# Attention heads of a hybrid layer: head output summed by VectorE from its bank, at other steps; query copy and key part moved by a step; value weights loaded in the fifth head

## The chip, the cores and the metric

The kernel runs on one core of a Trainium2 chip. The metric is the device time of one execution in microseconds, median of the runs of one kernel; less is better. All five engines have their own instruction stream: PE (TensorE), DVE (VectorE), ACT (ScalarE), POOL (GpSimd) and SP (SyncE, which here only issues transfers).

## The reference

One backbone layer over 512 latent tokens of 1024 channels and 256 context tokens. A combined projection feeds two branches: an eight-head attention with low-rank queries and keys (branch A), and a bidirectional gated linear attention with four heads (branch B). Their outputs are merged, added to the residual, and followed by a gated MLP with a 3x3 depthwise convolution. The change lies in branch A:

```python
s = jnp.einsum('bqhd,bkhd->bhqk', qn, k_nope) + jnp.einsum('bqhr,bkr->bhqk', qr, k_rope)
p = jax.nn.softmax(s.astype(jnp.float32) * MLA_SCALE, axis=-1).astype(v.dtype)
return jnp.einsum('bhqk,bkhd->bqhd', p, v)
```

There are 768 keys (512 latent, 256 context), 512 queries and 8 heads of 64 + 32 channels, values of 64 channels.

## The kernel before

All products run in float32 quality with operands split into two parts (`hi`, and `lo` = value minus `hi`): `mm3` is three matmuls, hi by hi, hi by lo and lo by hi. A split is a copy on ScalarE (`A`) and a subtraction on GpSimd (`G`) or VectorE (`V`).

The attention loop runs over heads `h` and six steps `s`. In each step the TensorE queue gets: four transposes of probabilities for the next step (`turned`, into one of two banks, copied by ScalarE to `ph` and subtracted by VectorE to `pl`), then what `between(h, s)` puts in, then `weighed`, four matmuls of the values of step `s` into the head's output bank `po`. `po` is `single[2]` for even heads and `single[3]` for odd ones. Its 128 rows hold 64 rows of the hi part of the value product and 64 of the lo part; the head's output is the sum of both halves, written as hi and lo into the rows of the head in `oT[pr]` (two heads share one tile).

`between` does, in the order of the code: exponentials of the scores made in the step before (`exped`, ScalarE), the second half of the key copy for the next pair of heads (`key_parts(1)`, ScalarE and VectorE, step 5 of even heads), the scores of the next head (`scores`, six matmuls into one of two double banks, and a row maximum on VectorE), the query product of the head after it (`prep_q`, in step 5 of even and step 0 of odd heads), the output of the head before (`heads_out`), the normalisation of probabilities (`normed`, a reciprocal on VectorE and a product on GpSimd), the key product of the next pair (`keys`, step 3 of even heads), and pieces of later work. `wide()` hands out the two double banks `two[0]` and `two[1]` in turn: to scores, key products and the query product of odd steps.

`prep_q` is a product (`q_mm`), a multiplication by a table on VectorE into the buffer `X` (`q_table`), and a split of `X` (`q_parts`, subtraction on GpSimd). `X` has one buffer, and `heads_out` uses it too:

```python
A.copy(hi, po[rw, :])
rest = tl(e1, [128, 512], F32, "X", 1)
A.copy(rest[rw, :], po[ro, :])
sub(V, lo, po[rw, :], f(hi))
tt(G, lo, f(lo), rest[rw, :], ALU.add)
```

`gla_v_load` loads the value weights of branch B (four loads of 512 KB), `gla_v_split` splits an eighth of them; `gla_steps` lists the step of each eighth. In head 7 the value product of branch B (`gla_v`) fills TensorE, in the two double banks.

During the attention the instructions of TensorE, VectorE and ScalarE stand in the order of the code. GpSimd's order, SP's, and everything after the attention is chosen by a planner from times of its own. Which buffer a tile of a pool gets is decided there too; a tile whose buffer is still in use waits for it. The tiles `s` of the trace have 30 buffers, `raw` 3, `whi` and `wlo` 4 each.

In the trace nearly all instructions show the line of a helper (L88), so the names of tiles tell them apart: `p` are the double banks, `pb` the single ones, `mx` the maxima, `rs` the row sums, `kT` the keys, `P` and `raw` the probabilities.

Of the kernel before, what the change touches and what calls it, by code (L numbers as in the profile page):

```python
# [9 lines left out]
F32 = mybir.dt.float32  # L10
# [3 lines left out]
ALU = mybir.AluOpType  # L14
# [6 lines left out]
NH = 8  # L21
# [49 lines left out]
def block_kernel(ctx: ExitStack, tc: tile.TileContext, p, out):  # L71
# [3 lines left out]
    class Engine:  # L75
# [5 lines left out]
        def __getattr__(self, op):  # L81
            fn = getattr(self.eng, op)

            def call(*args, **kw):
                if self.name in behind:
                    with tc.issue_after(behind[self.name].ins):
# [6 lines left out]
    V, A, G, PE, SY = (Engine("V", nc.vector), Engine("A", nc.scalar), Engine("G", nc.gpsimd),  # L93
                       Engine("PE", nc.tensor), Engine("SY", nc.sync))
    cnt = [0]

    def tl(pool, shape, dt, tag, bufs=None):
        cnt[0] += 1
        kw = {} if bufs is None else {"bufs": bufs}
        return pool.tile(shape, dt, name=f"{tag}_{cnt[0]}", tag=tag, **kw)  # L100
# [8 lines left out]
    def pb():  # L109
        return tl(psp, [128, 512], F32, "pb", 4)  # L110

    def p2():
        return tl(psp, [128, 1024], F32, "p2", 2)

    def S4(shape, dt=F32R):
        return tl(s4, shape, dt, "s4")

    def S4f():
        return S4([128, 1024], F32)
# [10 lines left out]
    def f(ap):  # L130
        return ap.bitcast(F32)

    def tt(eng, out_, a, b, op):
        return eng.tensor_tensor(out=out_, in0=a, in1=b, op=op)

    def sub(eng, out_, a, b):
        eng.tensor_tensor(out=out_, in0=a, in1=b, op=ALU.subtract)
# [6 lines left out]
    def mm3(o, sh, sl, mh, ml, first, last):  # L144
        PE.matmul(o, lhsT=sh, rhs=mh, start=first, stop=False)
        PE.matmul(o, lhsT=sh, rhs=ml, start=False, stop=False)
        return PE.matmul(o, lhsT=sl, rhs=mh, start=False, stop=last)
# [4 lines left out]
    def k3(t_, k, n):  # L152
        return t_[:, 0:k * n].rearrange("p (k n) -> p k n", k=k)
# [163 lines left out]
    def tok(kt, t):  # L317
        return lat(kt, t * 128, 128) if t < 4 else cxt(kt, (t - 4) * 128, 128)
# [16 lines left out]
    with tc.tile_pool(name="e1", bufs=1) as e1:  # L335
# [118 lines left out]
        def decay_weights():  # L454

            r, wd2 = S4f(), S4([128, 2, 512])
            for d in range(2):
                SY.dma_start(out=r[64 * d:64 * d + 16, 0:512], in_=p["gla_w_decay"][0, d])
            for d in range(2):
                yield  # L460
                rw = slice(64 * d, 64 * d + 16)
                G.tensor_copy(wd2[rw, 0, :], r[rw, 0:512])
                yield
                sub(G, wd2[rw, 1, :], r[rw, 0:512], f(wd2[rw, 0, :]))
                for n in range(3):
                    SY.dma_start(out=f(wst)[64 * d + 16 * n:64 * d + 16 * n + 16, :], in_=f(wd2)[rw, n % 2, :])
# [17 lines left out]
        two, single = [p2(), p2()], [pb() for _ in range(4)]  # L484
# [229 lines left out]
        def wide():  # L714
            turn[0] += 1
            return two[turn[0] % 2]

        def q_mm(h, qp):
            for k in range(3):
                mm3(qp, wqh[k][:, h, :], wql[k][:, h, :], qch[k], qcl[k], k == 0, k == 2)  # L720

        def q_table(qp):
            X = tl(e1, [128, 512], F32, "X", 1)
            tt(V, X, qp, qtab, ALU.mult)
            return X

        def q_parts(h, X):
            q2 = S4([128, 2, 512])
            A.copy(q2[:, 0, :], X)
            sub(G if h else V, q2[:, 1, :], X, f(q2[:, 0, :]))  # L730
            q2s[h] = q2

        def q_out(h, qp):
            q_parts(h, q_table(qp))

        def prep_q(h, qp):
            q_mm(h, qp)
            q_out(h, qp)
# [11 lines left out]
        def key_parts(i):  # L750
            kp = kps[0][64 * i:64 * i + 64, 0:768]
            A.copy(kTh[i][0:64, :], kp)
            sub(V, kTl[i][0:64, :], kp, f(kTh[i][0:64, :]))
# [14 lines left out]
        def scores(h, n):  # L768

            i, q2 = h % 2, q2s[h]  # L770
            cs = slice(n * 128, (n + 1) * 128)
            sp = wide()
            for (a, b) in ((0, 512), (512, 768)):
                mm3(sp[:, a:b], q2[:, 0, cs], q2[:, 1, cs], kTh[i][:, a:b], kTl[i][:, a:b], True, True)
            mx, rs = sm(1, "mx", 4), sm(1, "rs", 4)
            V.tensor_reduce(out=mx, in_=sp[:, 0:768], op=ALU.max, axis=AX.X, negate=True)
            pt = EP() if n < 2 else raw_tile()[:, 0:768]
            P[h].append(pt)
            open_.append((pt, rs, sp, mx))

        def exped():

            for pt, rs, sp, mx in open_:
                A.activation(pt, sp[:, 0:768], AF.Exp, bias=mx, accum_out=rs)
            exped_.extend(open_)
            open_.clear()

        def normed(n=4):

            for pt, rs, sp, mx in exped_[:n]:  # L790
                V.reciprocal(rs, rs)
                G.tensor_scalar(out=pt, in0=pt, scalar1=rs, scalar2=1.0, op0=ALU.mult, op1=ALU.mult)
            del exped_[:n]

        def heads_out(h, po):
            i, pr = h % 2, h // 2
            if i == 0:
                oT[pr] = S4([128, 2, 512])
            rw, ro = slice(64 * i, 64 * i + 64), slice(64 - 64 * i, 128 - 64 * i)
            hi, lo = oT[pr][rw, 0, :], oT[pr][rw, 1, :]  # L800
            A.copy(hi, po[rw, :])
            rest = tl(e1, [128, 512], F32, "X", 1)
            A.copy(rest[rw, :], po[ro, :])
            sub(V, lo, po[rw, :], f(hi))
            tt(G, lo, f(lo), rest[rw, :], ALU.add)

        def turned(h, s):

# [22 lines left out]
        glav, wv, gps, glv, m0 = [], [], {}, [None], []  # L831
# [3 lines left out]
        def gla_v_load(i):  # L835
            graw.append(S4f())
            SY.dma_start(out=k3(graw[i], 2, 512), in_=w_in[:, 2 * i:2 * i + 2, CGV:CGV + 512])

        def gla_v_split(k):

            if k % 2 == 0:
                whl_[:] = whl()
            wv.append([w[:, k % 2 * 512:k % 2 * 512 + 512] for w in whl_])
            split(*wv[k], graw[k // 2][:, k % 2 * 512:k % 2 * 512 + 512])
# [3 lines left out]
        def gla_v(t, k0=0, k1=KT):  # L848
            if k0 == 0:
                if t % 2 == 0:  # L850
                    glav.append(S4([128, 2, 512], F32))
                gps[t] = two[t // 2][:, t % 2 * 512:t % 2 * 512 + 512] if t < 4 else pb()
            for k in range(k0, k1):
                sh, sl = tok(k, t)
                glv[0] = mm3(gps[t], sh, sl, *wv[k], k == 0, k == 7)
            if k1 == KT:
                A.copy(glav[t // 2][:, t % 2, :], gps[t])

        def between(h, s):

            n = ((0, 1, 2, None, 3, None), (None, 0, 1, 2, 3, None))[h % 2][s]
            exped()
            if h + 2 < NH and (h % 2, s) == (0, 5):
                key_parts(1)
            if h + 1 < NH and n is not None:
                scores(h + 1, n)
            if h + 2 < NH and s == (5, 0)[h % 2]:
                prep_q(h + 2, wide()[:, 0:512] if h % 2 else single[3])
            if h > 0 and s == h % 2:
                heads_out(*pend)  # L870
            normed()
            if h + 2 < NH and (h % 2, s) == (0, 3):
                keys(h // 2 + 1)
                key_parts(0)
            if h == 2:
                next(dw, None)
            if h == 5 and 1 <= s <= 4:
                gla_v_load(s - 1)
            for k in range(KT):
                if (h, s) == gla_steps[k]:  # L880
                    gla_v_split(k)
            if (h, s) == (1, 2):
                pinned.add("G")
                misc_parts()
                pinned.discard("G")
            if h == 0 and s < 2:
                values(4 + s, single[3])
                values_out(4 + s, single[3])
            if (h, s) == (6, 5):
                begun.append(mp_tile())  # L890
                m0.append(mod_steps(3072, begun[0], raw_tile))
                next(m0[0])
                behind["SY"] = load[0]
            if h == 7:
                gla_v(*gla_fill[s])
                for _ in range(2 if s else 0):
                    next(m0[0], None)

        dw = decay_weights()
        gla_steps = [(5, 5), (6, 0), (6, 3), (6, 3), (6, 4), (6, 4), (6, 5), (6, 5)]  # L900
        gla_fill = [(0, 0, 2), (0, 2, 4), (0, 4, 6), (0, 6, 8), (1, 0, 4), (1, 4, 8)]

        cb_ = [single[1][:, 0:256], single[1][:, 256:512]]
# [119 lines left out]
        for h in range(NH):  # L1023
            po = single[2 + h % 2]
# [381 lines left out]
    with tc.tile_pool(name="eff", bufs=1) as ef:  # L1406
# [82 lines left out]
        for t in range(4):  # L1489
# [8 lines left out]
            for i, (a, b) in enumerate(parts):  # L1498
# [11 lines left out]
                else:  # L1510

                    cs = slice(t * 128, (t + 1) * 128)
                    rest = pb()[:, 0:256]
# [48 lines left out]
```

## Time and profile before

| | |
|---|---|
| median of 3 runs | 916.47 us (916.03 to 918.38) |
| profiled execution | 919.78 us |
| its span, first to last instruction | 918.0 us |
| mean granted TensorE clock | 0.994 |
| busy share PE / DVE / ACT / POOL | 97% / 63% / 44% / 42% |

The span is what the instructions take from the first to the last; the profiled execution's own time has 1.78 us around it. The attention loop lies between about 103 and 221 us of the span. A granted clock of 1.00 is TensorE's upper level (2.4 GHz), 0.50 its lower one (1.2 GHz).

### The profile page before, as it was taken

The numbers are of one execution on the slowest core, as the hardware profiler recorded it, in microseconds if no ns is written. First come the engines' busy times: TensorE is split into PE (matmuls) and PEld (weight loads), VectorE is DVE, ScalarE is ACT, GpSimd is POOL, SyncE is SP. The second block draws the span as 40 slices with busy tenths as digits, with TensorE's granted clock in tenths as the row PEclk, the third lists the DMA queues.
The fourth block names the chain that finished last, engine by engine and source line by source line (L and its number), as shares of the span: only waits on it lengthen the run. The fifth ranks groups of instructions, "written<-read, shape, count | busy, mean of one in ns | idle before, by whom it ended". The sixth has DMA issues, their size and how long they took to land.

```text
span 918.0 us, 12643 instructions
## 1 busy us (share of the span) xinstructions
PE 889.5 (97%) x4864; PEld 751.7 (82%) x4864; DVE 574.8 (63%) x963; ACT 399.9 (44%) x663; POOL 382.0 (42%) x231
## 2 busy tenths in 40 slices
PE   5999999989999999999999999999999999999996
PEld 4878888878878888888887889888888888888885
DVE  4567877664977777775665584988687776400006
ACT  4355666683435454533546333343424333322105
POOL 4412356472434443333464422344435344476403
PEclk9999999999999999999999999999999999999998
DMA  9930000306232424143982612434343433254102
GB/s 320 336 111 1 1 4 9 92 25 203 61 81 61 124 51 134 37 137 105 294 264 83 184 46 69 138 103 146 97 137 92 138 99 108 69 160 139 46 1 92
DMA packets 131437, 100.89 MB, mean 110 GB/s; under 512 B 6827, under 2 KB 121875, under 8 KB 131377
## 3 DMA queue, kind: packets, MB, share of 16 engines
q1 hardware_dynamic: 130256, 97.56, 34.8%
q0 software_dynamic: 864, 2.22, 0.7%
q8 instruction: 38, 0.62, 0.3%
q10 hardware_dynamic: 256, 0.30, 0.1%
q14 instruction: 23, 0.18, 0.1%
HBM read 97.78 MB, written 2.10 MB: 109 GB/s over the span
## 4 chain that ended last, share of the span: by engine, by line
PE 86%; DVE 5%; ACT 4%; issue 2%; POOL 1%; DMA 1%; POOLq 0%; DVEq 0%; ACTq 0%
PE pb L88 45%; PE p L88 22%; PE pb L87 14%; PE p L87 6%; DVE s L88 1%; DVE kT L88 1%; POOL s L88 1%; ACT ph L88 1%; DMA raw<-in_w_ada_dram 1%; ACT P L88 1%; DVE mx L88 1%; ACT s L88 1%; ACT raw L88 1%; DVE X L88 1%; ACT kT L88 1%
## 5 line engine op out<-in xcount | busy, mean ns | idle before, releaser
L88 POOL TENSOR_TENSOR wlo<-raw,whi 128x1024 fp32r<-128x1024 f32 (+1 forms) x106 | 240.9, 2279 | 338.8 <-ACT whi L88 310.3
L88 PE MATMUL pb<-s,whi 128*128 128x512 f32 (+1 forms) x906 | 272.3, 383 | 0.0
L88 PEld LDWEIGHTS pb<-s,whi 128*128 128x128 f32 x906 | 167.6, 188 | 32.2
L88 ACT CAST whi<-raw 128x1024 fp32r<-128x1024 f32 (+1 forms) x106 | 103.3, 975 | 178.0 <-issue 77.3
L88 PE MATMUL pb<-s,wlo 128*128 128x512 f32 (+1 forms) x453 | 172.9, 382 | 0.0
L88 DVE SCALAR_TENSOR_TENSOR ac<-pb,cwT,ac 128x441 f32<-128x441 f32 (+2 forms) x160 | 111.0, 694 | 19.3 <-ACT ac L88 15.4
L87 PE MATMUL pb<-s,whi 128*128 128x512 f32 x320 | 101.8, 396 | 0.0
L88 PEld LDWEIGHTS pb<-s,wlo 128*128 128x128 f32 x453 | 85.3, 188 | 16.5
L88 PE MATMUL p<-s,s 128*128 128x512 f32 (+1 forms) x392 | 83.5, 369 | 1.7 <-DVE s L88 1.7
L88 PEld LDWEIGHTS p<-s,s 128*128 128x128 f32 x392 | 66.4, 191 | 15.0 <-DVE s L88 2.3
L88 PE MATMUL p<-whi,s 128*128 128x512 f32 x208 | 69.9, 397 | 1.0 <-ACT raw L88 0.9
L87 PEld LDWEIGHTS pb<-s,whi 128*128 128x128 f32 x320 | 58.9, 188 | 12.4 <-issue 0.7
L88 DVE TENSOR_TENSOR p<-p,gt 128x512 f32<-128x512 f32 x4 | 2.8, 699 | 98.5 <-PE p L88 98.4
L87 PE MATMUL pb<-s,wlo 128*128 128x512 f32 x160 | 62.8, 392 | 0.0
L88 PE MATMUL pb<-whi,s 128*128 128x512 f32 x176 | 57.5, 390 | 0.0
L88 PEld LDWEIGHTS p<-whi,s 128*128 128x128 f32 x208 | 39.5, 190 | 9.6 <-ACT raw L88 1.1
L88 DVE TENSOR_TENSOR pl<-pb,ph 128x512 fp32r<-128x512 f32 x48 | 33.0, 687 | 20.0 <-ACT ph L88 19.9
L88 PE MATMUL p<-kT,s 128*128 128x512 f32 (+1 forms) x192 | 41.2, 351 | 3.6 <-ACT P L88 3.6
L88 PE MATMUL pb<-s,s 128*32 128x128 f32 (+2 forms) x322 | 43.6, 335 | 1.1 <-DMA s<-in_w_ada_dram 1.1
L88 PE MATMUL p<-wlo,s 128*128 128x512 f32 x104 | 41.0, 394 | 0.0
L88 ACT ACTIVATE ac<-ac 128x512 f32<-128x512 f32 x22 | 13.9, 632 | 60.8 <-DVE ac L88 60.8
L88 PE MATMUL p<-s,whi 128*128 128x256 f32 (+1 forms) x156 | 39.1, 342 | 1.3 <-DVE kT L88 1.2
(252 smaller groups left out, 1561.7 us busy)
## 6 DMA issues: line engine op xcount, KB each, us to landing
raw<-in_w_up_dram SPq DMA_DIRECT2D x44, 512.0 KB, 3.8
raw<-in_w_in_dram SPq DMA_DIRECT2D x28, 512.0 KB, 3.9
raw<-in_w_down_dram SPq DMA_DIRECT2D x22, 512.0 KB, 3.7
s<-in_w_ada_dram SPq DMA_DIRECT2D x20, 512.0 KB, 5.7
raw<-in_w_ada_dram SPq DMA_DIRECT2D x18, 512.0 KB, 4.8
xn<-in_w_ada_dram SPq DMA_DIRECT2D x10, 512.0 KB, 5.7
kT<-in_w_in_dram SPq DMA_DIRECT2D x8, 320.0 KB, 6.8
s<-in_x_dram SPq DMA_DIRECT2D x4, 512.0 KB, 5.1
```

Of the source, the lines that this page charges most:

```text
L87: return fn(*args, **kw)
L88: ins = fn(*args, **kw)
```

## The change

`heads_out` no longer copies the second half into `X`: VectorE adds it straight from the bank. It is called in step 2 of even heads (it was 0) and step 0 of odd heads (it was 1). `key_parts(1)` stands ahead of the exponentials of its step. In odd heads the query product and the table product stay in step 0, behind `heads_out`, and the split of `X` moves to step 1. The loads of the value weights move from steps 1 to 4 of head 5 to steps 2 to 5 of head 4, their splits from (5,5) to (6,5) to (4,5) to (6,3). The value product takes the two double banks in the other order.

```diff
-            rest = tl(e1, [128, 512], F32, "X", 1)
-            A.copy(rest[rw, :], po[ro, :])
             sub(V, lo, po[rw, :], f(hi))
-            tt(G, lo, f(lo), rest[rw, :], ALU.add)
+            tt(V, lo, po[ro, :], f(lo), ALU.add)
...
-                gps[t] = two[t // 2][:, t % 2 * 512:t % 2 * 512 + 512] if t < 4 else pb()
+                gps[t] = two[1 - t // 2][:, t % 2 * 512:t % 2 * 512 + 512] if t < 4 else pb()
...
+            even = h % 2 == 0
+            if h + 2 < NH and even and s == 5:
+                key_parts(1)
             exped()
-            if h + 2 < NH and (h % 2, s) == (0, 5):
-                key_parts(1)
             if h + 1 < NH and n is not None:
                 scores(h + 1, n)
-            if h + 2 < NH and s == (5, 0)[h % 2]:
-                prep_q(h + 2, wide()[:, 0:512] if h % 2 else single[3])
-            if h > 0 and s == h % 2:
+            if h + 2 < NH and even and s == 5:
+                prep_q(h + 2, single[3])
+            if h + 2 < NH and not even and s == 1:
+                q_parts(h + 2, X_[0])
+            if h > 0 and s == (2, 0)[h % 2]:
                 heads_out(*pend)
+            if h + 2 < NH and not even and s == 0:
+                qp = wide()[:, 0:512]
+                q_mm(h + 2, qp)
+                X_[0] = q_table(qp)
             normed()
...
-            if h == 5 and 1 <= s <= 4:
-                gla_v_load(s - 1)
+            if h == 4 and s > 1:
+                gla_v_load(s - 2)
...
-        dw = decay_weights()
-        gla_steps = [(5, 5), (6, 0), (6, 3), (6, 3), (6, 4), (6, 4), (6, 5), (6, 5)]
+        dw, X_ = decay_weights(), [None]
+        gla_steps = [(4, 5), (5, 0), (5, 2), (5, 3), (5, 4), (5, 5), (6, 0), (6, 3)]
```

## Rows read from the trace of the kernel before

**Rows 1.** Part 1 of the profile page: busy us of each engine, its share of the span, instructions.

```profile
PE 889.5 (97%) x4864; PEld 751.7 (82%) x4864; DVE 574.8 (63%) x963; ACT 399.9 (44%) x663; POOL 382.0 (42%) x231
```

**Rows 2.** Busy time by stretches: the stretch and its length, then busy us (and instructions) of PE, PEld, DVE, ACT and POOL, the granted clock, the DMA share and GB/s. The cuts are the first transposes of odd heads and of head 6, the start of head 7, the first value matmul and the end of the lower clock; the last row is all after the attention.

```profile
120.25:148.17 27.92, 26.68 (x176) 23.70 (x175) 20.29 (x35) 19.11 (x36) 19.75 (x20) 1.00 0.05 11
148.17:176.11 27.94, 26.71 (x176) 23.73 (x175) 20.30 (x35) 19.10 (x36) 12.38 (x12) 1.00 0.13 38
176.11:189.62 13.51, 12.31 (x83) 10.92 (x82) 10.01 (x17) 8.02 (x16) 6.54 (x6) 1.00 0.25 78
189.62:201.71 12.09, 10.50 (x74) 9.29 (x73) 8.47 (x16) 11.11 (x23) 9.85 (x10) 1.00 0.15 46
201.71:203.19 1.48, 0.60 (x6) 0.36 (x4) 1.03 (x3) 1.32 (x4) 1.48 (x2) 1.00 0.02 6
203.19:206.71 3.52, 3.52 (x10) 2.94 (x11) 0.84 (x2) 1.46 (x3) 3.52 (x4) 0.52 0.00 0
235.00:918.00 683.00, 674.02 (x3410) 567.83 (x3408) 422.41 (x668) 264.85 (x402) 286.25 (x129) 1.00 0.37 111
```

**Rows 3.** Who waited for whom, weight loads of TensorE (PEld) from 118 to 204 us: us in total, times, longest.

```profile
PEld p L88 <- ACT P L88: 5.2, 8, 1.2
PEld p L88 <- DVE kT L88: 1.9, 3, 0.6
PEld p L88 <- ACT raw L88: 1.1, 1, 1.1
PEld pb L88 <- DVE pl L88: 0.5, 1, 0.5
PEld pb L88 <- ACT ph L88: 0.5, 1, 0.5
```

**Rows 4.** The chain of work that ended last, 146 to 160 us (from the end of head 2 to the scores of head 3): start, us, engine and tile.

```profile
146.31 1.00 ACT raw L88 x2
...
147.33 0.81 ACT kT L88
...
148.16 0.97 DVE kT L88
...
151.01 1.25 POOL s L88
...
155.05 0.58 ACT X L88
...
157.19 1.32 PE p L88 x6
```

**Rows 5.** TensorE in order of time, one step of head 3: start, us (the ends are modelled and overlap the next start), what; the first row of each group (transposes, query product, weighing, transposes, scores, weighing).

```profile
148.17 0.60 PE L88 MATMUL pb<-cst,P 128*128 128x128 f32 x4
149.17 0.74 PE L88 MATMUL p<-s,whi 128*128 128x512 f32 x2 [0.40 <-DVE kT L88]
...
151.38 0.28 PE L88 MATMUL pb<-ph,s 128*128 128x256 f32 x1
...
151.85 0.60 PE L88 MATMUL pb<-cst,P 128*128 128x128 f32 x4
152.21 1.30 PE L88 MATMUL p<-kT,s 128*128 128x512 f32 x6
153.34 0.29 PE L88 MATMUL pb<-ph,s 128*128 128x256 f32 x1
...
155.80 0.60 PE L88 MATMUL pb<-cst,raw 128*128 128x128 f32 x4
```

**Rows 6.** VectorE and GpSimd in order of time: a row maximum and the subtraction for the output of head 1 (136.12, 137.10; the output lies in the upper half of the partitions), the table product into X, a maximum, the subtraction for the output of head 2 (lower half) and the next instruction, and GpSimd's addition for that output.

```profile
136.12 0.95 DVE L88 TENSOR_REDUCE mx<-p 128x1 f32<-128x768 f32 x1
137.10 0.69 DVE L88 TENSOR_TENSOR s<-pb,s 64x512 fp32r<-64x512 f32 x1
...
152.30 0.69 DVE L88 TENSOR_TENSOR X<-p,qtab 128x512 f32<-128x512 f32 x1 [0.48 <-POOL s L88]
...
154.78 0.95 DVE L88 TENSOR_REDUCE mx<-p 128x1 f32<-128x768 f32 x1
155.66 0.68 DVE L88 TENSOR_TENSOR s<-pb,s 64x512 fp32r<-64x512 f32 x1
156.28 0.69 DVE L88 TENSOR_TENSOR pl<-pb,ph 128x512 fp32r<-128x512 f32 x1
...
156.43 1.28 POOL L88 TENSOR_TENSOR s<-s,X 64x512 fp32r<-64x512 f32 x1 [1.41 <-DVE s L88]
```

**Rows 7.** The chain of work that ended last, the last piece before the first value matmul of branch B, which is the end of the last score's exponential: start, us, engine and tile.

```profile
202.95 0.20 ACT raw L88
```

**Rows 8.** SP's queue in order of time around the loads of the value weights (`s<-in_w_in_dram`) and the load behind them; the last row is that of the transfers, from 165 to 185 us: KB each, median us from issue to landing.

```profile
170.88 0.40 SPq L88 DMA_DIRECT2D s<-in_w_in_dram  x1
172.87 0.39 SPq L88 DMA_DIRECT2D s<-in_w_in_dram  x1
178.56 0.88 SPq L88 DMA_DIRECT2D s<-in_w_in_dram  x2
198.78 0.37 SPq L88 DMA_DIRECT2D raw<-in_w_ada_dram  x1
s<-in_w_in_dram SPq DMA_DIRECT2D x4, 512.0 KB, 3.8
```

**Rows 9.** Who waited for whom, TensorE from 235 us to the end: us in total, times, longest.

```profile
PE p L87 <- ACT T L88: 1.0, 1, 1.0
```

## The prediction, made before the changed kernel ran

> **What bounds the kernel now.** I read the busy shares first: TensorE has work for 97% of the span [rows 1]. So the change can only win time in which TensorE stands still, or runs at its lower clock, and only in the attention that it touches. The next view is the busy time by stretches [rows 2]. I cut the attention at the first transposes of odd heads. Heads 1 and 2 take 27.92 us, heads 3 and 4 take 27.94, head 5 takes 13.51, head 6 takes 12.09. Then come 1.48 us before the first matmul of the linear-attention values, and 3.52 us at a granted clock of 0.52, which is the lower of the two levels (1.2 GHz); before and after it is 1.00 (2.4 GHz).
>
> How much of this is waiting? The starts of TensorE's groups in one step tell what each piece takes when nothing holds it [rows 5]: a query product 149.17 to 151.38, 2.21 us; the weighing by the values 0.47; four transposes 0.36; six score matmuls 152.21 to 153.34, 1.13. A key product streams as many columns as a query product (4608 by the code), so 2.21. A pair of heads is 8 scores, 12 transposes, 12 weighings and 3 products: 9.04 + 4.32 + 5.64 + 6.63 = 25.63 us. It takes 27.94, so 2.31 us of it is waiting. Head 5 alone is 4.52 + 2.16 + 2.82 + 2.21 = 11.71 of 13.51, so 1.80 waiting; head 6 has no product left, 9.50 of 12.09, so 2.59. With 1.12 us ahead of the value matmuls (1.48 less one 0.36) the waits are 2 x 2.31 + 1.80 + 2.59 + 1.12 = 10.1 us. The view of who waits for whom, for the weight loads, names 9.2 of them [rows 3]: 5.2 for exponentials (ACT P), 1.9 in three places for the key copy (DVE kT), 1.1 for the last exponential (ACT raw), 1.0 for the transposes' copies (ph, pl).
>
> The chain of waits says where one pair's waits come from [rows 4]. ScalarE copies the keys at 147.33, behind an exponential of 1.00 us that started at 146.31. VectorE subtracts until 149.13, and only then is the bank free for the next query product (transposes at 148.17, product at 149.17, so 0.64 us lost [rows 5]). GpSimd's subtraction 151.01 + 1.25 for query part h holds the one X buffer, so VectorE's next table product starts at 152.30 [rows 6], though the matmuls had ended at 151.38. The copy of the query, the second GpSimd subtraction and ScalarE's copy of the head's second half into that same X buffer (155.05) follow. The exponential behind that copy ends after 157, and TensorE starts its scores at 157.19 [rows 4]; its transposes were through at 155.80 + 0.36 = 156.16. That is 1.03 us. The rest of a pair, 2.31 - 0.64 - 1.03 = 0.64, lies in small waits of the even head.
>
> **The change part by part.** *Head output.* One ScalarE copy (0.58) and one GpSimd addition (1.28, [rows 6]) go for each head, and VectorE gets an addition of the form of its subtraction next to it. That one has its next neighbour started 0.62 us later (155.66 to 156.28) for the output of an even head [rows 6]. A read of the other half of the bank is not in the trace; its bounds are 0.62 and, with no overlap at all with the neighbours, 0.69 + 0.1 on either side, 0.9. I take 0.65, as the ScalarE copy that crosses halves is no longer (0.58) than its neighbour. VectorE is busy 20.30 of 27.94 us in a pair [rows 2] and gets 2 x 0.65 = 1.3, so 21.6, 83% of a pair shortened to 25.9; it stays off the path unless it is late with a row maximum. The X buffer no longer carries this half, so the wait of ScalarE for GpSimd goes.
>
> One row speaks against it: the subtraction behind a row maximum of 0.95 us starts 0.88 after it in the one case (154.78 to 155.66) and 0.98 after it, when the maximum has ended, in the other, where the output lies in the upper half of the partitions (136.12 to 137.10) [rows 6]. The Trainium skill has a rule for it (VectorE: DVE Perf Modes, section "Two Vector instructions with no wait between them"): an instruction whose input or output starts in another 32-partition quadrant than the last one's waits until all earlier Vector instructions have ended. By it the new addition and its follower would both be held, some 0.2 us a head and 1.4 us of VectorE over seven heads; where VectorE is the later engine (head 6) the sum would be about 0.3 us worse. By the rows alone the hold is 0.10 each and inside the 0.9 bound above.
>
> *Key copy ahead of the exponential.* kT moves in front of 1.00 us of exponential [rows 4], so its subtraction ends near 148.1, and the query product can follow its transposes at 148.17 + 0.36 = 148.53. The table product of the other query starts some 1.0 us earlier too, and the GpSimd subtraction behind it ends near 151.24. What is late by this is the exponential (0.8 us, the length of the copy [rows 4]); its bank is wanted only at the second next score, after a 2.21 us product, so it costs nothing; without that product in between it would cost the 0.8.
>
> *Head output in step 0 (odd) and 2 (even), query copy in step 1.* I carry the order on each engine through with these durations. Query product 148.53 to 150.74. VectorE: the transposes' subtraction until 150.6, head output's subtraction and addition until 151.9, table product until 152.5, the next transposes' subtraction until 153.1, the maximum of the first score (matmuls 151.5 to 152.7) until 154.0. ScalarE: query copy at 152.6, transposes' copy at 153.9, the first score's exponential from 154.35 until 155.4. The second score starts at 153.5; the third, which needs the first one's bank, at 155.49. So the 1.03 us wait goes, with 0.1 us of margin. Carried on through the even head, one wait of about 0.2 us is left at its third score, and the period is 25.9 us. That is 2.0 us a pair, 4.0 for two. What queues behind the new addition is the maximum of the next score, and with it the exponential and the next but one score; a table product 0.1 us later shows there at once.
>
> *Value weights earlier.* Eight casts on ScalarE and eight subtractions on GpSimd of 128x512, now in heads 5 and 6, move to the end of head 4 up to head 6. The four loads of 512 KB go first. In the trace they start at 170.88, when the last key product has ended, at 172.87 and at 178.56, wherever a buffer comes free, and land in 3.8 us [rows 8]. On SP's queue the next one behind them is a load at 198.78, so they are moved past nothing; no transfer of GpSimd's queue is passed. The last key product ends some 5 us before the first cast is due, so 3.8 us are covered. If the buffer is another, see below. With one cast in a step, head 5 keeps waits near 0.5 us and one of 0.2 (the output buffer of heads 4 and 5, which I expect free only after the last query product): 1.80 - 0.7 = 1.1 won. Head 6 has seven casts now and two then, but VectorE, 8.47 busy of 12.09 [rows 2] and 0.65 more, becomes the later engine: 0.25 won.
>
> *Bank of the value matmuls.* Now they take the bank of the last score, whose exponential ends at 202.95 + 0.20 [rows 7]. The other bank has been free since the score before. This wins the 1.12 us. Behind this wait TensorE ran at the lower clock for 3.52 us [rows 2]. The six value matmuls (6/9 of 2.21) and one weighing in it are 1.47 + 0.47 = 1.94 us at the full clock, so 1.58 us come back if the clock does not fall. Nothing says at which gap it falls; I count all of it, and keep the loss as a rival.
>
> **Sum.** 4.0 + 1.1 + 0.25 + 1.12 + 1.58 = 8.05, say 8.1 us. The profiled execution took 919.78 us (span 918.0, 1.78 around it), so 911.7 for it; its median of the runs shown is 916.47, 3.31 less, so the forecast is 916.47 - 8.1 = 908.4 us. After the attention TensorE waits 1.0 us in 683 [rows 2, 9], so an earlier end of the attention is an earlier end of all.
>
> **The rivals.**
> *The clock falls anyway.* Head 6 keeps some 2 us of short waits by my count. If they are enough, 1.58 comes back: 910.0. For it: 2.59 us of waits there now, and the fall just behind. Against: the longest gap, 1.12, is gone. 14%.
> *VectorE becomes the bound.* The added 0.65 to 0.9 us stands in front of a maximum in each head; margin 0.1. If it shows in seven heads: 7 x 0.7 = 4.9 back, 913.3. For it: 83% busy, in order. Against: the table products come 1.0 us earlier. 10%.
> *ScalarE waits for the value weights.* If the first load gets its buffer only after head 5's query product, as the third and fourth do now (178.56), the cast stands for about 2.9 + 3.8 - 1.3 = 5.4 us with the transposes' copies behind it: 913.8. Against: a buffer came free at 170.88 already. 7%.
> *The bank swap does nothing* (the last score lies in the other bank after all): 1.12 + 1.58 lost, 911.1. Against: the number of scores and products that alternate between the two is unchanged. 3%.
> *Slower.* The order after the attention is the planner's, made from its own times, and it may come out otherwise. If VectorE or ScalarE then held TensorE in each of the four linear-attention heads, 2.8 us a head would eat the 8.1 and 2.8 more: 919.3. For it: nothing pins that order. Against: 1.0 us of waits in all of it now, VectorE 422 of 683 busy [rows 2, 9]. It decides from 2.8 us a head on. 4%.
> My forecast has the other 62%.
>
> **Range.** All waits gone would be 10.1 + 1.58 = 11.7: 904.8. The upper end takes in the clock, the swap and the VectorE case: 913.3. A measurement tells 0.3% (2.75 us) from no change; faster by that is below 913.7. The forecast, clock, swap and most of the VectorE case are on that side: 0.86; the third rival and the rest about 0.09; slower 0.05.
>
> **What would show it.** In the profile after: no weight-load wait for kT, pairs near 25.9 us, no X copy on ScalarE, GpSimd's 64x512 addition gone, two VectorE rows s<-pb,s for each head, value casts from head 4 on, clock 1.00 through the first value matmuls. Wrong if pairs stay above 27, if a row "ACT whi <- DMA" appears in head 4, if waits for maxima (DVE mx) take over, or if TensorE's waits after the attention exceed 3 us.

## The result: faster by 6.9 us, less than forecast, and not for all the reasons given

| | before | after |
|---|---|---|
| median of five runs each, same chip | 918.38 us (916.03 to 919.51) | 911.5 us (909.66 to 913.15) |
| ratio, 95% interval | | 0.9926, 0.9908 to 0.9944 |
| profiled execution, span | 919.78, 918.0 | 913.15, 911.4 |

The interval is 5.1 to 8.4 us won; the forecast was 8.1 won, as 908.4. The time lies 3.1 us above that: 1.9 because the kernel before ran at 918.38 here and not at 916.47, the rest because less was won.

Part 1 of the page of after (as [rows 1]):

```profile
PE 886.5 (97%) x4864; PEld 750.7 (82%) x4864; DVE 580.1 (64%) x971; ACT 396.3 (43%) x655; POOL 372.6 (41%) x223
```

VectorE has eight instructions more (one for each head), ScalarE and GpSimd eight fewer each. The same stretches as in [rows 2], of after (columns as there: length, busy us of PE, PEld, DVE, ACT, POOL, granted clock, DMA share, GB/s): two pairs of heads, head 5, head 6, the gap before the first value matmul, the first value matmuls with one weighing, the rest.

```profile
121.54:147.41 25.87, 25.87 (x176) 23.64 (x175) 21.52 (x37) 18.18 (x35) 17.23 (x18) 1.00 0.05 12
147.41:173.25 25.84, 25.84 (x176) 23.59 (x175) 21.54 (x37) 18.15 (x35) 9.85 (x10) 1.00 0.27 81
173.25:186.78 13.53, 12.25 (x84) 10.87 (x82) 9.73 (x18) 9.98 (x21) 11.20 (x10) 1.00 0.01 2
186.78:197.79 11.01, 10.32 (x74) 9.33 (x73) 9.00 (x16) 9.11 (x19) 7.46 (x8) 1.00 0.15 49
197.79:198.15 0.36, 0.36 (x7) 0.36 (x5) 0.36 (x2) 0.24 (x1) 0.36 (x2) 1.00 0.17 54
198.15:200.10 1.95, 1.95 (x14) 1.69 (x11) 1.14 (x3) 1.86 (x4) 1.28 (x2) 1.00 0.00 0
200.10:911.37 711.27, 702.15 (x3552) 591.29 (x3550) 439.67 (x695) 276.37 (x421) 287.93 (x131) 1.00 0.37 113
```

The pairs took 27.92 and 27.94 [rows 2] and take 25.87 and 25.84: TensorE is busy in all of them. Head 5 took 13.51 and takes 13.53: nothing was won there. Head 6 fell from 12.09 to 11.01, the gap from 1.48 to 0.36. Who waited for whom, weight loads of after, 118 to 198 us (as [rows 3]):

```profile
PEld p L88 <- ACT P L88: 1.5, 4, 0.7
PEld pb L88 <- POOL P L88: 1.2, 1, 1.2
PEld pb L88 <- DVE pl L88: 0.5, 1, 0.5
```

9.2 us have become 3.2. The key copy and the last exponential are gone from the list, the waits for exponentials fell from 5.2 to 1.5, and one wait is new: for GpSimd's normalisation (POOL P).

VectorE of after in order of time, in the stretch of head 3 that the prediction walked through (`pl` is the subtraction for the transposes):

```profile
149.97 1.40 DVE L88 TENSOR_TENSOR s<-pb,s 64x512 fp32r<-64x512 f32 x2
151.40 0.69 DVE L88 TENSOR_TENSOR X<-p,qtab 128x512 f32<-128x512 f32 x1
152.01 0.68 DVE L88 TENSOR_TENSOR pl<-pb,ph 128x512 fp32r<-128x512 f32 x1
152.61 0.95 DVE L88 TENSOR_REDUCE mx<-p 128x1 f32<-128x768 f32 x1
```

Subtraction and addition of the head output, table product, the transposes' subtraction and the first maximum follow one another with no idle time between them. The prediction's walk started 0.76 us later, at 148.17 against 147.41. With that taken off, table product and maximum started within 0.3 us of where it put them, and the exponential (153.59) on the spot. The one wait that it left, about 0.2 us at the third score of the even head, is there too: the weight loads wait 0.16 for an exponential at 137.81 and again at 163.65.

### The profile page after: what moved, and what is told of

It reads as the page before. It is cut to its first block, busy times and chain, and to the rows that moved or that the text cites. A ratio compares the mean times of both kernels' runs of the same rounds, so it can differ in the third digit from the quotient of the medians.

```text
span 911.4 us, 12634 instructions
## 1 busy us (share of the span) xinstructions
PE 886.5 (97%) x4864; PEld 750.7 (82%) x4864; DVE 580.1 (64%) x971; ACT 396.3 (43%) x655; POOL 372.6 (41%) x223
## 4 chain that ended last, share of the span: by engine, by line
PE 90%; DVE 4%; ACT 2%; issue 1%; POOL 1%; DMA 1%; SPq 0%; DVEq 0%; ACTq 0%; POOLq 0%
PE pb L88 47%; PE p L88 23%; PE pb L87 14%; PE p L87 6%; DVE s L88 1%; DMA raw<-in_w_ada_dram 1%; DVE kT L88 1%; ACT s L88 1%; ACT P L88 0%; DVE P L88 0%; DVE mx L88 0%; ACT kT L88 0%; POOL P L88 0%; POOL s L88 0%; POOL wlo L88 0%
## 5 line engine op out<-in xcount | busy, mean ns | idle before, releaser
L87 PEld LDWEIGHTS pb<-s,whi 128*128 128x128 f32 x320 | 58.9, 188 | 12.4 <-issue 0.7
L88 PEld LDWEIGHTS pb<-s,s 128*128 128x128 f32 (+1 forms) x322 | 34.1, 166 | 6.4 <-DVE rv L88 1.1
```

The costliest lines, as they stand in the source:

```text
L87: return fn(*args, **kw)
L88: ins = fn(*args, **kw)
```

## The experiments

Each kernel is compared with runs of the kernel before on its own chip. Some are the kernel after with one part undone, some the kernel before with one part done.

**u_keys: `key_parts(1)` behind the exponentials again.**

```diff
-            if h + 2 < NH and even and s == 5:
-                key_parts(1)
             exped()
+            if h + 2 < NH and even and s == 5:
+                key_parts(1)
```

> The changed kernel with one part undone: the second half of the key copy stands behind the exponentials of its step again. Theory (the exponential in front of the copy holds the bank of the next query product): the wait of 0.6 us for kT is back in three places and the table product is 1.0 us later, so a pair of heads takes 26.5 to 26.9 us instead of 25.9, and the whole 1.9 to 3 us more than the changed kernel. Rival (VectorE, with its new addition, is the later one, and the place of the key copy is hidden): pairs stay at 25.9 to 26.0, the whole within 0.3 us.

Measured: 915.29, ratio 0.9976 (0.9956 to 0.9996). One pair and head 5 by stretches:

```profile
120.00:146.87 26.87, 26.40 (x177) 23.66 (x175) 21.52 (x37) 18.17 (x34) 17.24 (x18) 1.00 0.04 11
...
173.69:188.22 14.53, 12.84 (x83) 10.95 (x82) 10.62 (x18) 9.91 (x20) 11.15 (x10) 1.00 0.01 4
```

The view of who waits for whom, weight loads, has the keys back as in [rows 3]:

```profile
PEld p L88 <- DVE kT L88: 1.9, 3, 0.6
```

Undoing this part alone costs 1.00 and 0.98 us in the two pairs and 1.00 in head 5, 3.0 in all; the pairs are as the theory had them. The weight loads' wait is 0.64 of each. Most of the other third is a wait of 0.27 of the third score of head 3 for its exponential (at 155.10, none in after): the table product and the first maximum behind the keys come later too (the maximum starts 6.21 us after the head's first transposes, 5.20 in after).

**u_out: head output by ScalarE's copy and GpSimd's addition again, at the new steps.**

```diff
+            rest = tl(e1, [128, 512], F32, "X", 1)
+            A.copy(rest[rw, :], po[ro, :])
             sub(V, lo, po[rw, :], f(hi))
-            tt(V, lo, po[ro, :], f(lo), ALU.add)
+            tt(G, lo, f(lo), rest[rw, :], ALU.add)
```

> The changed kernel with one part undone: the head's second half is copied by ScalarE into X and added by GpSimd again, at the new steps. Theory (the one X buffer and ScalarE's wait for it were the larger wait of a pair): the addition on GpSimd now stands in front of the table product of the odd heads, so a pair takes 27.1 to 27.7 us, and the whole 4 to 5.5 us more than the changed kernel. Rival (the gain of a pair came from the key copy and the new steps): pairs at 26.2 or less, the whole under 1 us more.

Measured: 917.88, ratio 0.9997 (0.9982 to 1.0012). The pairs take 27.69 and 27.73, at the upper end of the theory's range, and head 5 becomes 3 us longer, head 6 0.67 (stretches):

```profile
173.71:190.22 16.51, 13.80 (x83) 12.28 (x82) 9.13 (x17) 10.68 (x22) 12.43 (x11) 0.90 0.01 4
190.22:201.90 11.68, 10.44 (x75) 9.26 (x74) 8.77 (x15) 9.63 (x20) 8.70 (x10) 1.00 0.15 48
```

A good half of the 3 us in head 5 is the clock: its mean is 0.90 there, by an estimate 1.65 us (0.10 of 16.51).

TensorE in order of time, the first scores of head 3:

```profile
152.65 1.32 PE L88 MATMUL p<-kT,s 128*128 128x512 f32 x6 [1.13 <-DVE X L88]
```

Here the copy into `X` and GpSimd's addition stand ahead of the table product that wants `X`, and TensorE waits 1.13 us for it (2.13 in head 5). The new steps need the new way of summing.

**b_out: the kernel before with VectorE's addition alone, at the old steps** (the edit of u_out, the other way round).

> The kernel before with one part of the change alone: VectorE adds the head's second half straight from the bank; every step stays where it was. Theory (the X buffer and ScalarE's wait for it cost 1.0 us per odd head): pairs of heads go from 27.9 to 26.7 to 27.1 us, the kT wait of 0.6 stays, the whole 2.5 to 4 us less than before. Rival (the key copy's place decides a pair): pairs at 27.5 or more, the whole within 1 us.

Measured: 922.03, ratio 1.0045 (1.0027 to 1.0063): slower. The pairs take 29.29 and 29.20, 1.3 more than before. Neither side expected this: the theory had a gain, and the rival the whole within 1 us. VectorE in order of time in head 3:

```profile
156.30 0.95 DVE L88 TENSOR_REDUCE mx<-p 128x1 f32<-128x768 f32 x1
157.17 1.40 DVE L88 TENSOR_TENSOR s<-pb,s 64x512 fp32r<-64x512 f32 x2
158.60 0.69 DVE L88 TENSOR_TENSOR pl<-pb,ph 128x512 fp32r<-128x512 f32 x1
159.21 0.95 DVE L88 TENSOR_REDUCE mx<-p 128x1 f32<-128x768 f32 x1
```

ScalarE, the exponential behind the second maximum:

```profile
160.19 0.90 ACT L88 ACTIVATE P<-p,mx 128x768 f32<-128x768 f32 x1 [1.44 <-DVE mx L88]
```

TensorE, the score that wants this exponential's bank:

```profile
161.24 0.96 PE L88 MATMUL p<-kT,s 128*128 128x512 f32 x3 [0.66 <-ACT P L88]
```

At the old step the two instructions stand between two row maxima. The second maximum comes 2.91 us after the first, its exponential waits 1.44 for it, and the score that wants that bank waits 0.66 more.

**b_own: the kernel before with a buffer of its own for the second half instead of `X`** (in bfloat16, so that this half is rounded).

```diff
-            rest = tl(e1, [128, 512], F32, "X", 1)
+            rest = tl(e1, [128, 512], mybir.dt.bfloat16, "rest", 1)
```

> The kernel before with one edit: ScalarE copies the head's second half into a buffer of its own instead of X (kept in bfloat16, for there is no room for more); GpSimd still adds it. Theory (it is the wait for the buffer that costs): pairs at 26.8 to 27.2 us, as with VectorE's addition alone. Rival (it is ScalarE's and GpSimd's time for the two instructions): pairs at 27.6 or more.

Measured: 917.05, ratio 0.998 (0.9964 to 0.9995). A pair by stretches:

```profile
120.18:147.86 27.68, 26.77 (x176) 23.74 (x175) 20.14 (x35) 19.23 (x36) 19.55 (x20) 1.00 0.05 11
```

ScalarE no longer waits for the buffer, and a pair still takes 27.68: 0.24 of the 1.03 us is won, as the rival had it. In the kernel before that wait was 0.44 us long (ScalarE in order of time):

```profile
155.05 0.58 ACT L88 COPY X<-pb 64x512 f32<-64x512 f32 x1 [0.44 <-POOL s L88]
```

The chain through `X` [rows 4] ended last, but right behind it stood another that ended almost as late: ScalarE's own order. In b_own the query copy waits for the table product, and from it on copies stand in a row up to the first exponential, with no more than 0.03 us between them; the third score still waits 0.44 for that exponential (156.50), where it waited 0.79:

```profile
152.73 0.62 ACT L88 CAST s<-X 128x512 fp32r<-128x512 f32 x1 [1.94 <-DVE X L88]
```

The reason given for those 1.03 us falls. The next theory was that the order of the steps makes the gain; two kernels take one step each back.

**r_h1: after, with the head output at the old steps.**

```diff
-            if h > 0 and s == (2, 0)[h % 2]:
+            if h > 0 and s == h % 2:
```

> The changed kernel with one part undone: the head output is back at step 1 of odd and step 0 of even heads, still added by VectorE from the bank. New theory (the two instructions, 1.4 us, then stand between two maxima instead of in VectorE's idle time beside the query product): pairs at 26.6 to 27.6 us instead of 25.9, the whole 1.5 to 4 us more than the changed kernel. Rival (the query copy's step alone gives it): pairs at 26.1 or less.

Measured: 919.36, ratio 1.0007 (0.9989 to 1.0024). A pair, as the theory had it, and head 6, 0.69 longer than in after, by stretches:

```profile
120.10:147.65 27.55, 26.35 (x176) 23.64 (x175) 21.70 (x37) 18.12 (x35) 17.17 (x18) 1.00 0.04 11
188.68:200.38 11.70, 10.67 (x74) 9.35 (x73) 8.99 (x16) 9.45 (x19) 8.29 (x9) 1.00 0.13 39
```

VectorE in head 3, where the two instructions again stand between two maxima (152.55 and 155.45):

```profile
153.41 1.40 DVE L88 TENSOR_TENSOR s<-pb,s 64x512 fp32r<-64x512 f32 x2
```

**r_q0: after, with the query split back in step 0.**

```diff
-            if h + 2 < NH and not even and s == 1:
-                q_parts(h + 2, X_[0])
...
-                X_[0] = q_table(qp)
+                q_parts(h + 2, q_table(qp))
```

> The changed kernel with one part undone: in odd heads the split of X (the query copy on ScalarE) is back in step 0, straight behind the table product. New theory, after the two runs on the kernel before (the wait of a pair is made by order: ScalarE's copy of the next transposes stands behind the query copy, and so behind the table product, and the first maximum comes late): the first maximum of an odd head ends 0.8 to 1.2 us later, and a pair takes 26.5 to 27.0 us instead of 25.9. Rival (the head output's step alone gives it, as VectorE does it while the query product runs): pairs at 26.1 or less.

Measured: 917.98, ratio 1.0007 (0.9991 to 1.0022). Head 5 takes 15.28, 1.75 more than in after. A pair by stretches, just above the theory's range:

```profile
119.98:147.08 27.10, 26.22 (x176) 23.65 (x175) 21.62 (x37) 17.94 (x35) 17.23 (x18) 1.00 0.05 11
```

ScalarE in head 3, the copy of the query and what stands behind it:

```profile
151.79 0.62 ACT L88 CAST s<-X 128x512 fp32r<-128x512 f32 x1 [2.32 <-DVE X L88]
152.32 1.07 ACT L88 CAST ph<-pb 128x512 fp32r<-128x512 f32 x2
```

TensorE, the third score:

```profile
155.56 1.31 PE L88 MATMUL p<-kT,s 128*128 128x512 f32 x6 [0.82 <-ACT P L88]
```

The copy of the query waits 2.32 us for the table product, and the transposes' copies, behind it in ScalarE's order, come only at 152.32. In after the first of these runs ahead of the query's, at 151.09.

So the gain of a pair hangs on all four parts, the steps among them: on the mean of both pairs the old step of the head output costs 1.68 us, that of the query split 1.22, the old place of the keys 0.99, the old way of summing 1.86. Their sum is 5.7 where 2.1 were won. They don't add up, because each alone lets another of the chains end last: the maxima in r_h1, the query copy in r_q0, the key copy in u_keys, the table product in u_out.

**u_bank: the value product's banks in the old order.**

```diff
-                gps[t] = two[1 - t // 2][:, t % 2 * 512:t % 2 * 512 + 512] if t < 4 else pb()
+                gps[t] = two[t // 2][:, t % 2 * 512:t % 2 * 512 + 512] if t < 4 else pb()
```

> The changed kernel with one part undone: the value product takes the bank of the last score again. All theories: the wait of about 1.1 us ahead of the first value matmul is back. Theory A (the fall of the clock came from this wait): the stretch behind it runs at the lower level again, 1.6 us more, 2.7 us in all. Theory B (it came from the sum of waits in head 6, of which there are fewer now): the clock stays at 1.00 and the whole is 1.1 us more.

Measured: 914.66, ratio 0.9964 (0.9948 to 0.9979). Stretches, the gap and the value matmuls behind it:

```profile
196.82:198.31 1.49, 0.60 (x6) 0.36 (x5) 0.99 (x3) 1.29 (x4) 1.13 (x2) 1.00 0.08 25
198.31:200.28 1.97, 1.97 (x11) 1.71 (x11) 1.62 (x4) 0.90 (x2) 1.46 (x2) 1.00 0.00 0
```

The 1.13 us are back, and in this execution the clock does not fall behind them. **b_again** is the kernel before, profiled once more to see whether it falls there.

> The kernel before once more, unchanged, for its profile. If the fall of the clock in front of head 7's value matmuls belongs to this order of work, the stretch behind the 1.1 us wait is at the lower level again (3.5 us instead of 1.95). If it depends on where the waits fall in time from one execution to the next, it is at 1.00 here, as in the two kernels with the same wait that kept it.

The same two stretches:

```profile
201.67:203.16 1.49, 0.60 (x6) 0.36 (x4) 1.03 (x3) 1.33 (x4) 1.49 (x2) 1.00 0.02 7
203.16:205.13 1.97, 1.97 (x10) 1.71 (x11) 0.62 (x2) 1.46 (x3) 1.97 (x3) 1.00 0.00 0
```

Span 916.4, run 918.2, 1.6 less than the profile that the prediction read: the same wait, and 1.97 us at full clock where there were 3.52 at 0.52 [rows 2]. Of five profiles with that gap (before, b_again, b_out, b_own, u_bank) only the first shows the fall. That the first was one of the longer executions can be seen in the runs: of the 66 runs of the kernel before beside these experiments, the 24 with a mean granted clock of 0.994, as in the first profile, all took 919.52 us or more, and the 42 with 0.995 or 0.996, as in b_again, 919.35 or less. Where in the 24 the clock was lower was not recorded.

**u_values: value weights loaded and split at the old steps.**

```diff
-            if h == 4 and s > 1:
-                gla_v_load(s - 2)
+            if h == 5 and 1 <= s <= 4:
+                gla_v_load(s - 1)
...
-        gla_steps = [(4, 5), (5, 0), (5, 2), (5, 3), (5, 4), (5, 5), (6, 0), (6, 3)]
+        gla_steps = [(5, 5), (6, 0), (6, 3), (6, 3), (6, 4), (6, 4), (6, 5), (6, 5)]
```

> The changed kernel with one part undone: loads and splits of the value weights at their old steps in heads 5 and 6. Theory (in the changed kernel GpSimd's subtractions of value weights stand in front of a normalisation at the end of head 5, 1.2 us of wait): head 5 takes 12.0 to 12.4 us instead of 13.5, head 6 goes back to 12.1 from 11.0, so this part of the change wins nothing by itself, 0 to 0.5 us either way, unless the clock falls behind head 6, then 1.6 us more. Rival (the early splits are what won head 6 and hold nothing in head 5): head 5 stays at 13.3 to 13.5, the whole 1.1 us or more above the changed kernel.

Measured: 914.47, ratio 0.9956 (0.9937 to 0.9975). Head 5, head 6 and the rest by stretches:

```profile
172.12:183.92 11.80, 11.80 (x84) 10.91 (x83) 9.77 (x18) 7.63 (x16) 5.28 (x5) 1.00 0.30 93
183.92:195.45 11.53, 10.49 (x75) 9.32 (x74) 9.05 (x17) 10.52 (x22) 7.67 (x8) 1.00 0.16 48
...
197.76:913.61 715.85, 704.47 (x3552) 592.76 (x3550) 439.94 (x695) 276.81 (x423) 292.85 (x135) 1.00 0.37 112
```

Without the value weights head 5 has no wait left (11.80, the 11.71 of the prediction's count), head 6 gets 0.52 longer and not the 1.1 that both sides expected, and the rest 4.6. So this part lost 1.7 us in head 5 and won 0.5 in head 6; the rest of what it won is 0.9 in head 7, and 3.7 in one place at 243 us (last section). The theory's 0 to 0.5 us for the whole missed these.

**n_pool and n_steps: what head 5 waits for.** After's GpSimd in order of time in head 5:

```profile
181.55 0.92 POOL L88 TENSOR_SCALAR P<-P,rs 128x768 f32<-128x768 f32 x1 [1.06 <-DVE rs L88]
182.43 2.55 POOL L88 TENSOR_TENSOR wlo<-s,whi 128x512 fp32r<-128x512 f32 x2
184.94 0.93 POOL L88 TENSOR_SCALAR P<-P,rs 128x768 f32<-128x768 f32 x1
```

After's TensorE, the transposes that want these probabilities:

```profile
185.91 0.55 PE L88 MATMUL pb<-cst,P 128*128 128x128 f32 x3 [1.00 <-POOL P L88]
```

The reciprocal of the second normalisation ended at 183.65. GpSimd's order is the planner's, and it put two subtractions of value weights, 2.55 us, ahead of it. n_pool takes GpSimd from the planner from step 4 of head 4 to the end of the attention, so that its instructions stand in the order of the code:

```diff
+            if (h, s) == (4, 4):
+                pinned.add("G")
...
-    pinned -= {"V", "A"}
+    pinned -= {"V", "A", "G"}
```

n_steps has this edit and other steps for the splits, two of them in head 7:

```diff
-        gla_steps = [(4, 5), (5, 0), (5, 2), (5, 3), (5, 4), (5, 5), (6, 0), (6, 3)]
+        gla_steps = [(4, 4), (4, 5), (5, 2), (5, 4), (6, 3), (6, 5), (7, 0), (7, 1)]
```

> The changed kernel with GpSimd kept in the order of the code from step 4 of head 4 on, so that the normalisation of a step stands in front of the subtraction of value weights of the same step. Theory (the wait of 1.2 us at the last transposes of head 5 is GpSimd's order): head 5 takes 12.3 to 12.6 us instead of 13.5, the whole 0.9 to 1.2 us less than the changed kernel. Rival (VectorE's reciprocal is late anyway): head 5 stays at 13.2 or more.

> The changed kernel with GpSimd in the order of the code as in the run before it, and the eight splits of the value weights at other steps: (4,4), (4,5), (5,2), (5,4), (6,3), (6,5), (7,0), (7,1), the last two beside the value matmuls of head 7, where ScalarE and GpSimd have room. Theory (casts and subtractions in successive steps make the waits left in heads 5 and 6): head 5 12.0 to 12.3 us, head 6 10.4 to 10.8, the whole 1.5 to 2.5 us less than the changed kernel. Rival (VectorE bounds head 6): head 6 stays at 11.0.

Measured: n_pool 910.92, ratio 0.9924 (0.9903 to 0.9945); n_steps 908.31, ratio 0.9898 (0.988 to 0.9917). Head 5 of n_pool by stretches:

```profile
172.91:185.25 12.34, 12.05 (x84) 10.89 (x83) 9.68 (x18) 9.98 (x21) 9.95 (x9) 1.00 0.01 4
```

Its GpSimd in order of time there:

```profile
182.09 1.29 POOL L88 TENSOR_TENSOR wlo<-s,whi 128x512 fp32r<-128x512 f32 x1
183.42 0.91 POOL L88 TENSOR_SCALAR P<-P,rs 128x768 f32<-128x768 f32 x1
```

Heads 5 and 6 of n_steps by stretches:

```profile
171.95:184.29 12.34, 12.05 (x83) 10.89 (x82) 9.69 (x18) 8.97 (x19) 7.82 (x7) 1.00 0.02 6
184.29:194.81 10.52, 10.22 (x75) 9.32 (x74) 8.97 (x17) 8.18 (x17) 5.88 (x7) 1.00 0.17 51
```

With one subtraction ahead of it the normalisation starts at 183.42 and head 5 takes 12.34: 1.19 us, the whole wait for POOL. n_steps takes another 0.50 out of head 6.

The whole times do not all show what the stretches show. The table has the difference to the changed kernel, once by the ratios (an estimate from the two intervals makes each good to some 2.5 us), once by the stretches of the one profile, from the first transposes of head 1 to the end:

| | expected | by ratios | by stretches |
|---|---|---|---|
| u_keys | 1.9 to 3 | 4.6 | 3.0 |
| u_out | 4 to 5.5 | 6.5 | 7.3 |
| u_bank | 1.1, or 2.7 with a fall of the clock | 3.5 | 1.1 |
| u_values | 0 to 0.5 | 2.8 | 3.3 |
| r_h1 | 1.5 to 4 | 7.4 | 7.6 |
| r_q0 | no figure | 7.4 | 6.3 |
| n_pool | -0.9 to -1.2 | -0.2 | -1.1 |
| n_steps | -1.5 to -2.5 | -2.6 | -1.7 |

So n_pool's 1.2 us is shown in head 5 and not in the whole time, and u_bank's ten runs lie further above the changed kernel than its one profile accounts for; why is open.

## Why the prediction was right and wrong

Term by term, against b_again, whose clock did not fall:

| | forecast | measured |
|---|---|---|
| two pairs | 4.0 | 2.03 + 2.08 = 4.1 |
| head 5 | 1.1 | 0.0 |
| head 6 | 0.25 | 1.1 |
| wait before the value matmuls | 1.12 | 1.13 |
| clock behind it | 1.58 | 0.0 |
| sum | 8.05 | 6.3 |

6.3 lies in the measured interval, 5.1 to 8.4. Against the first profile, in which the clock did fall, the same stretches give 7.9 of the 8.05. That closeness is luck: head 5 was 1.1 too high and head 6 0.85 too low, and the fall belongs to some executions only.

*The pairs: right in size, half wrong in cause.* Carrying each engine's order through with durations of the trace gave 25.9, and it was 25.87. Where the step gave a reason instead, it failed: it laid 1.03 us to the `X` buffer and GpSimd's hold of it, since the chain of waits went that way. b_own takes that away and wins 0.24. The chain shows the one sequence that ended last; it doesn't say how late the next is. The walk had all of them in it, the query copy's order too, so its number survived the wrong reason; of the number itself little is luck, as starts and the one wait left agree.

*The keys: right, and under-read.* The copy was laid at 0.64 in the weight loads; undone, it costs 1.0 in each of three places.

*The head output on VectorE: the cost inside its bounds, its bearing missed.* With both instructions in place the table product starts 1.43 us after the subtraction (149.97 to 151.40), where the follower of the subtraction alone started 0.62 after it [rows 6]: 0.81 more, between the 0.65 taken and the bound of 0.9. The Trainium skill (VectorE: DVE Perf Modes, "Two Vector instructions with no wait between them") has instructions that change quadrant held until the earlier ones have ended; the trace agrees, 0.70 for each of the two and 0.03 of idle time behind them. The rival of VectorE as the bound has the right mechanism for another kernel: in b_out and r_h1, at the old steps, the addition stands between two maxima, and b_out's pairs are 1.3 us longer than with the old way of summing. At the new steps a maximum stands behind it as well, with no idle time between, but no wait of a matmul follows: they are busy for all of the 25.87 us.

*Head 5: the step that failed.* The prediction took one cast in a step for ScalarE and never put GpSimd's subtractions in order with GpSimd's normalisations. What it named as possibly late (a load, the output buffer) was not: no wait for a transfer shows, and n_pool shows the 1.2 us to be the order on GpSimd. With that order put right head 5 takes 12.34, where the forecast's 13.51 - 1.1 is 12.4: the rest of the count for this head holds. The statement that GpSimd's order is the planner's stood in the description of the kernel and was not used.

*Head 6: mis-sized, 1.1 for 0.25.* VectorE was named as the later engine; it is busy 9.00 of 11.01 and TensorE waits 0.27 for it at one place. The prediction also looked only at the casts of value weights, and they are half of it: undone, they cost 0.52 (u_values), while the old way of summing costs 0.67 (u_out) and the old step of the head output 0.69 (r_h1). The largest wait, for an exponential, fell from 0.98 to 0.42, and is 0.44 in u_values, so the value weights are not what shortened it. What is left are waits of 0.42 (exponential), 0.27, and short ones.

*The bank: right to 0.01.*

*The clock: a term read from one execution.* The fall is not fixed to the wait; it was priced in full and held with a rival that only asked whether other waits would keep it. The question to ask was whether the kernel before has it in each execution, and the prediction had a sign: the profiled execution took 919.78 us, its three other runs 916.03 to 918.38.

*The rivals.* The loads of value weights were issued from 158.02 on and no cast waited for one. The order after the attention came out as good: 711.27 us behind the first value matmuls against 711.28 in b_again. In the rival that it might not, 2.8 us in each of four heads is 11.2 and not 8.1 + 2.8; nothing hangs on it.

## What to carry to other kernels

When several engines run in a written order, walk all of them through with durations of the trace: that gave 25.9 where it was 25.87, and the chain of waits alone gave a wrong cause, because it names the last sequence and not the one right behind it. List every engine that gets moved work, also those whose order nobody wrote, and ask at each wanted instruction what now stands ahead of it. A move of work to another engine can be worth nothing or less without the move of its place, as b_out and u_out show from both sides; and a cost seen in one execution, such as a fall of the clock, should be looked for in a second before it is counted.

## What the runs showed of the hardware that was not expected

**A gap is followed by a fall of the clock in some executions only.** Behind 1.1 us of standing still ahead of the value matmuls it fell in one profile of five. Three kernels have a wait of 1.79 us at about 245 us; behind it the clock fell in u_values and r_h1, not in r_q0. In u_out it fell behind a wait of 2.13 us in head 5 (0.50 from 183.00 to 185.00), not behind the 1.13 in head 3. The stretch in u_values, 0.51, which is the lower level (1.2 GHz):

```profile
245.25:248.60 3.35, 3.35 (x16) 3.17 (x16) 1.25 (x4) 0.79 (x2) 0.09 (x1) 0.51 0.34 102
```

**VectorE and GpSimd take turns.** The waits of 1.79 us are waits for VectorE. Its multiply-adds of the modulation, before GpSimd's subtractions of weights and beside them, in after (the view of one tile: count, then ns min/median/max, first and last start):

```profile
L88 DVE SCALAR_TENSOR_TENSOR mp<-s,csilu,mp x5: 484/485/485, 232.3 to 234.4; 128x256 f32<-128x256 f32 x5
...
L88 DVE SCALAR_TENSOR_TENSOR mp<-s,csilu,mp x4: 2608/2612/2630, 235.0 to 242.6; 128x256 f32<-128x256 f32 x4
```

GpSimd's subtractions in after, in order of time:

```profile
234.81 10.17 POOL L88 TENSOR_TENSOR wlo<-raw,whi 128x1024 fp32r<-128x1024 f32 x4 [33.74 <-ACT whi L88]
```

0.485 us become 2.61, one for each of GpSimd's four of 2.5 us. The Trainium skill (GPSIMD Engine Reference, section "1. Specifications") says that the two share their SBUF interfaces, with "contention with DVE instructions in a 2-port perf mode or with two SBUF inputs"; the multiply-adds have two (`s` and `mp`), and the trace agrees, at 2.1 us an instruction. In after the plain product between them, 0.35 us, got through just ahead of the block; in u_values it did not, and took 2.58. It has one tensor input, and no run shows whether it falls under the other case. After:

```profile
234.76 0.35 DVE L88 TENSOR_SCALAR mp<-s,csilu 128x256 f32<-128x256 f32 x1
```

u_values:

```profile
233.35 2.58 DVE L88 TENSOR_SCALAR mp<-s,csilu 128x256 f32<-128x256 f32 x1
```

TensorE's wait for these products in u_values:

```profile
243.56 0.61 PE L88 MATMUL pb<-ones,mp 128*128 128x1 f32 x4 [1.79 <-DVE mp L88]
```

Behind it, in two kernels, the clock costs some 1.6 more (0.49 of the 3.35 in u_values). VectorE starts its product 0.05 us ahead of the block in after and 0.02 in u_values, so some of what u_values, r_h1 and r_q0 lost (2.0 to 3.7 us) hangs on hundredths of a microsecond and is no merit of the steps. That was read from traces and not tried by an edit; the contention as the cause of the longer instructions is argued from their one-to-one pairing.

**The start moves.** The change begins in the attention, and yet the first transposes of head 1 come between 118.29 (u_out) and 121.54 us (after). Part of it is the first matmul, which waits 4.18 (u_bank) to 5.40 us (b_own) for its input; another is a wait of 1.25 us for VectorE at about 75 us, which all of them show but u_out. What decides these is not shown: the planner's order ahead of the attention may differ too. So the spans of two profiles compare to some 3 us only, and the parts above are taken from stretches.
